# Gating a chunk of the mLSTM behind the first head of the next chunk

## The chip, the cores and the metric

The kernel runs on one core of a Trainium2 chip. The metric is the device time of one execution in microseconds (us), the median of several runs. Five engines run side by side, each with its own queue of instructions in a fixed order: PE (TensorE, matrix products, with weight loads shown apart as PEld), DVE (VectorE), ACT (ScalarE), POOL (GpSimd) and SP (SyncE, which issues most loads). ACT issues the stores.

## The reference, cut to what matters

The reference is one step of a two-layer streaming encoder. The change touches one part of layer 0, the mLSTM mixer over 16 meta tokens and 2048 prompt tokens, with 4 heads of 256 features:

```
h = num / jnp.maximum(jnp.abs(den), jnp.exp(-m))[..., None]     # per head, a row per token
...
C1 = decay[..., None, None] * C0 + jnp.einsum('bhsd,bhse->bhde', kw, v)   # state after the chunk
...
y = head_norm(h, norm_w) + skip.astype(F32) * xc
...
gated = jnp.concatenate([ya * jax.nn.silu(za), yb * jax.nn.silu(zb)], axis=-1)
```

So each token's rows are normed per head, scaled by `norm_w`, the product of `skip` and the convolved input `xc` is added (the skip product), and all of it is multiplied by the gate `zb`.

## The kernel before

The prompt is worked in chunks of 128 tokens. `phase_mlstm` (from 925 to about 1250 us of the profile) takes one unit of the meta tokens and then eight units of two chunks. In the texts below A is the first chunk of a unit and B the second. Pass i of the loop writes the score stage of unit i+1 (`ml_scores`), and then the heads of A and of B of unit i (`ml_heads`), each followed by its gating (`ml_gated`).

- **Score stage** (needs no state). `xc` is split in two float32r parts (L105 on ACT, L106 on POOL). The queries of the unit are 48 products (L111, L112, L113, 16 of each) in four PSUM tiles, copied out by ACT (L1092). For each chunk: a load of the decay rows `rw` (L1108, SP) and of the values `va` (L1114), the scaled queries `qs` (L1117, two on DVE), the keys turned in two PSUM tiles (L1125) and weighted into `kw` by ACT (L1128), the weights `w` (L1132 on ACT, L1133 on POOL), the scores in one PSUM tile (L1142) and their weighting into `p` (L1145, DVE), and last the skip product `g` (L1147, POOL).
- **Heads**, four per chunk. Products L1272 and L1274 give the head's rows in a PSUM tile `pn`; L1277 gives two tiles `pc` by which DVE (L1281) moves the state `ct`. `ml_normed` takes statistics on DVE (L1158 to L1164), a power on POOL (L1165, L1166), and ACT writes the normed rows into `yn` (L1167).
- **Gating** of a chunk. SP loads `zb` (L1175). Two groups of four turns on PE (L1180, heads 0 and 1, then 2 and 3) go to two PSUM tiles, read by two groups of four DVE instructions (L1183) that add into `g`. POOL multiplies `g` by `zb` (L1185), ACT stores (L1186).

PSUM tiles are lent by name. `pa` has three slots, shared by the four query tiles, the six tiles of keys and scores of a unit, and the four tiles of its gating; `pn` has three and `pc` two. In SBUF `yn`, `g` (`m_g`), `kw`, `p`, `qs`, `rw` and `zb` have two slots each, `xc` three: a chunk's `yn` can be written only when the chunk two before it has been turned, and its `g` only when L1185 of the chunk two before it is through. In units 2 to 5 a row of out-projection weights is staged in a slot of `zb` (L1320 to L1322); the last loads of weights (L1312) and the operands of the first tile of the out-projection take slots of `xc`.

The order of instructions in each engine's queue is not the written order. The framework lays the queues out at build time: among instructions whose operands and slots are there, the one written earlier goes first. So where a step is written decides who gets a slot that comes free, and the layout is fixed before the program runs.

Of the kernel before, what the change touches and what calls it, by code (L numbers as in the profile page):

```python
# [9 lines left out]
F32 = mybir.dt.float32  # L10
# [3 lines left out]
OP = mybir.AluOpType  # L14
# [9 lines left out]
KD = 8  # L24
# [21 lines left out]
def opn(e, name, bufs=1, side=None, psum=False):  # L46
    """open a pool that outlives the function; cls closes it"""
    if psum:
        cm = e.tc.tile_pool(name=name, bufs=bufs, space=MemoryType.PSUM, side=side, reuse_waits="tile")
    else:  # L50
        cm = P(e, name, bufs, side)
    e.cms[name] = cm
    return cm.__enter__()
# [11 lines left out]
def exp_acc(nc, pool, out, x, shape, nm):  # L65
    """out = exp(x) to float32 accuracy; x is clobbered."""
# [19 lines left out]
def log1p_acc(nc, pool, out, z, shape, nm):  # L86
    """out = log(1 + z) for 0 <= z <= 1."""
    s = pool.tile(shape, F32, name=nm + "_s")
    q = pool.tile(shape, F32, name=nm + "_q")
    p = pool.tile(shape, F32, name=nm + "_p")  # L90
    v = nc.vector
    v.tensor_scalar(s, z, 2.0, None, op0=OP.add)
    v.reciprocal(s, s)
    v.tensor_mul(s, s, z)
    v.tensor_mul(q, s, s)
    v.tensor_scalar(p, q, 1.0 / 17.0, None, op0=OP.mult)
    for k in (15.0, 13.0, 11.0, 9.0, 7.0, 5.0, 3.0):
        v.scalar_tensor_tensor(p, p, 1.0 / k, q, op0=OP.add, op1=OP.mult)
    v.scalar_tensor_tensor(out, p, 1.0, s, op0=OP.add, op1=OP.mult)
    v.tensor_scalar(out, out, 2.0, None, op0=OP.mult)  # L100


def split(nc, h, l, x, pool=False, act=True):
    """x = h + l with both parts exact in float32r."""
# [4 lines left out]
def mm3(nc, out, a, b, start, stop, **kw):  # L109
    """out (+)= a.T @ b with operands split in two parts; a, b: (h, l) tuples of APs."""  # L110
# [5 lines left out]
def token_tiles():  # L116
    """(column of the first token, tokens, kind, row)"""
# [17 lines left out]
def params(e, ps):  # L135
    """Per-feature vectors and conv histories, one row each, turned to feature-major columns."""
# [32 lines left out]
def rms_rstd(e, out, junk, x, n):  # L169
    """out [n, 1] = (mean(x^2) + eps)^-1/2 over the rows of x [n, 1024]; junk: room for the squares"""  # L170
# [6 lines left out]
def norm_u(e, ps, x, n, rs, nwb, uh, ul, pname, pbufs, keep=None):  # L177
    """x [n, 1024] token-major -> x * rs * nwb (in place), feature-major in two parts: uh, ul [128, 8, n]; keep takes
    them, half of the features at a time"""
# [13 lines left out]
def blocks_of(first, rest):  # L193
    """token tiles in blocks of tiles: (tiles, first column, columns)"""
# [8 lines left out]
def phase_in0(e):  # L203
    """norm of layer 0, S5 input and its gate; weight preparation beside it"""
# [5 lines left out]
    with P(e, "a_w") as wp, P(e, "a_sb", 2) as sb, PS(e, "a_ps") as ps:  # L210
# [37 lines left out]
        for i, bi in enumerate(seq):  # L248
# [33 lines left out]
            if i == 4:  # L282
                # the first columns of what follows
# [10 lines left out]
def prep_ml(e, sb, ps):  # L294
    """mLSTM projections folded: q~ = xc (wq wk^T) / 16, gate weights on xc and on xb"""
    nc = e.nc
    # gate weights of two heads side by side, in 32 rows each of which 8 count
# [43 lines left out]
def phase_l0(e):  # L341
    """xb, zb of layer 0, conv, values, gates; S5 beside it; the mLSTM factors"""
# [13 lines left out]
    def mtile(third, m, isz, ut, pg, parts):  # L356
        """a generator: the first block of tokens, then the rest"""
# [52 lines left out]
        # four parts side by side in the array  # L410
# [4 lines left out]
    def quarters(ut):  # L415
        """(first column, columns) of the parts of a third, from its start"""
# [3 lines left out]
    def values(h, ut, tiles, parts):  # L420
        """token-major values of a head, and what they add to the gates"""
# [32 lines left out]
    for third in range(3):  # L454
# [6 lines left out]
        if third > 0:  # L461
            # the second block takes the room of the last third's first
# [7 lines left out]
        def tile(m, isz):  # L470
            """values wait for one more tile, till their operands are split"""
# [71 lines left out]
def s5_open(e, ps):  # L543
    """discretised S5: powers of A, coefficients of B (stacked: real part over imaginary part), states"""
# [4 lines left out]
    with P(e, "s5prm", side="right") as sb:  # L549
# [52 lines left out]
        # (A - 1) / lambda  # L602
# [20 lines left out]
        # by position in the chunk: the last one has power 0  # L623
# [10 lines left out]
        # B as stored [g, p, c] -> [p twice, g, c]  # L634
# [6 lines left out]
        # states of the running streams, stacked  # L641
# [13 lines left out]
def s5_u(e, sb, q):  # L655
    """S5 input of 4 groups: rows (position, channel), two halves of 8 positions each, per group and chunk"""
# [7 lines left out]
def s5(e, ps):  # L664
    """a generator: l0 takes a piece at a time"""
# [5 lines left out]
    with P(e, "s5a", side="right") as sb:  # L671
# [31 lines left out]
        # states of the running streams  # L703
# [18 lines left out]
        # scan over the chunks of the prompt: pairs of chunks first, then the chunks between  # L722
# [8 lines left out]
        def advance(dst, src, n, g0):  # L731
            """ee[dst] += A^16 ee[src] for n chunks, every second one"""
# [39 lines left out]
    with P(e, "s5y", side="right") as sb:  # L772
        # coefficients of C; C as stored [g, c, p] -> [p twice, (g c)]; skip weights on the diagonal of lag 0
# [15 lines left out]
        # four groups of lags lie side by side in 32 rows each, the upper 16 unused  # L789
# [55 lines left out]
    # gelu, GLU, gate; the weights in the room of the normed tokens' rows  # L845
    with P(e, "s5g", side="right") as sb:
# [24 lines left out]
        def operands(b):  # L871
            """4 of the 16 positions, half the chunks"""
# [39 lines left out]
def gate_rows(e, ps):  # L912
    """running max and decay sums of the mLSTM gates; rows (slot, head): slot 0 the running streams, 1 the meta
    tokens, 2.. the chunks of the prompt. Leaves every chunk's factors."""
    nc, v = e.nc, e.nc.vector
    with P(e, "gr", side="right") as sb:
# [29 lines left out]
        # running max over the chunks of the prompt  # L946
# [3 lines left out]
        # turned to one row per head and one column per chunk, and back  # L950
# [48 lines left out]
def m_open(e, ps):  # L999
    """mLSTM factors and weights, while the in-projection still runs"""  # L1000
# [34 lines left out]
def ml_scores(e, sb, lp, hp, pt, slots):  # L1035
    """everything of a chunk that needs no state: values, queries, weighted keys, weighted scores; lp: the pool of
    what is loaded; hp: the pool of what is dropped at the end; pt: PSUM tiles by use"""
    nc, v = e.nc, e.nc.vector
    sk = e.row["ml_skip"]
# [16 lines left out]
    else:  # L1056
        kt = xc
        am = e.m.am
        if meta:
            # apart, that the next chunks' need not wait  # L1060
# [5 lines left out]
    if meta:  # L1066
        # few tokens: the weights run, and the queries are turned
# [34 lines left out]
    for i, slot in enumerate(slots):  # L1102
# [8 lines left out]
        # values with columns of ones  # L1111
# [34 lines left out]
        g = c.g = sb.tile([128, KD, 128], F32, name="m_kt" if dec else "m_g", bufs=nb(2))  # L1146
        nc.gpsimd.tensor_tensor(g[:, :, :n], c.xc, e.pc[:, :, sk:sk + 1].to_broadcast([128, KD, n]), op=OP.mult)  # L1147
# [3 lines left out]

def ml_normed(e, c, h, pn):
    """a head's rows over their normaliser, normed"""
# [16 lines left out]
def ml_gated(e, c):  # L1170
    """norm weights, gate"""
# [17 lines left out]
def ml_running(e, sb, pt):  # L1189
    """the running streams, each with its own state; a generator of one step per head and four streams. Two streams  # L1190
    fill 32 columns of the array, so that four products run side by side."""
# [5 lines left out]
    # keys and values, split  # L1197
# [8 lines left out]
    for h in range(H):  # L1206
# [6 lines left out]
        for b in range(2):  # L1213
# [12 lines left out]
            # two streams fill 32 rows of the array as well, one of them masked  # L1226
# [24 lines left out]
def ml_columns(e, sb, ptile, src, name):  # L1251
    """normaliser states out, from columns"""
# [12 lines left out]
def ml_heads(e, c):  # L1265
    """a chunk's rows, and the state after it"""
    nc, ct, n = e.nc, e.m.ct, c.n
    first = c.slot == 1  # the streams of the prompt start from nothing
# [15 lines left out]
    ml_gated(e, c)  # L1284


def phase_mlstm(e):
# [5 lines left out]
    def weights(k, r, h, l):  # L1293
        """of the out-projection"""
# [3 lines left out]
    with P(e, "m_sb", 2) as sb, PS(e, "m_ps") as ps:  # L1298
# [3 lines left out]
        nxt = ml_scores(e, sb, lp, ow0, pt, units[0])  # L1302
        for i in range(len(units)):
# [3 lines left out]
            else:  # L1307
                # the rest of the weights in the room of the last chunks' queries and keys
# [7 lines left out]
            for c in cur:  # L1316
                ml_heads(e, c)
            if 2 <= i < 6:
                # staged in line with the gates
                r = sb.tile([128, D], F32, name="m_zb", bufs=2)  # L1320
                nc.sync.dma_start(r, out_w(e)[:, i - 2, :])
                weights(i - 2, r, *(ow0.tile([128, D], F32R, name=f"wo{x}{i - 2}") for x in "hl"))  # L1322
        t = out_tiles(e)[0]
# [6 lines left out]
        # state of the prompt in the basis of k  # L1330
# [14 lines left out]
def split_weights(e, wp, src, ks, width, name, stg, sname, bufs=2):  # L1345
    """DRAM matrix [128, k, width] -> its two parts, a tile per k"""
# [16 lines left out]
def out_tiles(e):  # L1363
    """token tiles in the order of the out-projection; the meta tokens go apart"""
# [4 lines left out]
def out_operands(e, room, parts, c0, n, kind, row):  # L1369
    """gated tokens, split; room(j, "g" or "h" or "l"): tiles for a part of the features"""  # L1370
# [22 lines left out]
def phase_out0(e):  # L1393
    """out-projection of layer 0, residual; the first in-projections of layer 1"""
# [3 lines left out]
    with P(e, "o_sb", 2) as sb, P(e, "o_w") as wp:  # L1398
# [22 lines left out]
        def meta():  # L1421
            """few tokens: a quarter of the features each, side by side in the array; a generator of a step per k"""
# [20 lines left out]
        # two tiles at once while the weights come  # L1443
# [45 lines left out]
def p1_block(e, b):  # L1489
    """room for the normed tokens of a block"""  # L1490
# [35 lines left out]
def p1_plain(e, m, wt, b):  # L1526
    """128 columns of q, k, v (m < 16) or of the gate of the retention, for a block of tokens"""
# [11 lines left out]
def phase_in1(e):  # L1539
    """in-projection of layer 1; RG-LRU as its inputs come"""  # L1540
# [6 lines left out]
    with P(e, "p_ms") as sb:  # L1547
        cs = sb.tile([128, KD, 27], F32, name="p_cs", bufs=1)
        hs = sb.tile([128, KD, 9], F32, name="p_hs", bufs=1)
        # softplus(-lambda) = max(-lambda, 0) + log1p(exp(-|lambda|)), times 2 for the tanh below  # L1550
# [15 lines left out]
        # the first columns run block by block, as the normed tokens come  # L1566
# [103 lines left out]
        def values(j, wv):  # L1670
            """512 columns of v, token-major; the first block as it comes, then turned"""
# [55 lines left out]
def phase_ret(e):  # L1727
    """retention, out-projection of layer 1, final norm"""
# [3 lines left out]
    # the last columns of the in-projection run block by block; the room of the finished blocks goes to what follows  # L1732
# [25 lines left out]
    def retention(c0, n, kind, row):  # L1758
        """-> the gated parts, split, for the out-projection"""
# [26 lines left out]
        if not meta:  # L1786
# [8 lines left out]
            for h in range(H):  # L1795
                po = ps.tile([128, 256], F32, name="r_o", bufs=2)
                mm3(nc, po, hd(p, h), hd(vv, h), True, False, skip_group_check=dec)
                if dec:
                    # two streams fill 32 columns of the array: four products run side by side
# [94 lines left out]
    def load(j, ks):  # L1894
        """weights of the out-projection; those of the RG-LRU come first"""
# [146 lines left out]
```

## Time and profile before

| what | value |
|---|---|
| three runs, us | 3164.87, 3166.68, 3168.04 (median 3166.68) |
| span of the profiled execution, first to last instruction | 3164.7 us |
| PE busy over the span | 3012.2 us (95%) |
| DVE busy over the span | 1725.9 us (55%) |
| mean granted TensorE clock over the span | 0.979 of full speed |
| the mLSTM phase, 925 to 1260 us | PE busy 302.17 of 335, DVE 251.31, POOL 180.40 |

The page gives the profiled execution's span and no other time of its own; the span lies 0.2 us under the lowest of the three runs and 2.0 us under their median. A busy PE is not PE at its peak, since the ends of pipelined matmuls are modelled. "L1183" is line 1183 of the kernel before.

### The profile page before, as it was taken

What the parts mean: (1) busy time and instruction counts of PE and PEld (TensorE: products, weight loads), DVE (VectorE), ACT (ScalarE), POOL (GpSimd) and SP (SyncE); (2) the same over time, 40 slices, a digit from 0 to 9 for tenths busy, and PEclk for the clock granted to TensorE, in tenths of its full rate; (3) what the DMA queues carried; (4) which work ended last, traced back from release to release, by engine and by line L of the source; (5) the groups of instructions that cost most, each with busy time, mean ns of one, the idle gap of its engine ahead of it and who ended that gap; (6) DMA issues with size and microseconds to landing.
All of it is one profiled execution on the core that took longest, in us unless ns stands there. A gap on an engine that the chain in (4) does not pass through costs nothing.

```text
span 3164.7 us, 45082 instructions
## 1 busy us (share of the span) xinstructions
PE 3012.2 (95%) x17427; PEld 2721.5 (86%) x17427; DVE 1725.9 (55%) x3449; ACT 1059.3 (33%) x1860; POOL 905.3 (29%) x931
## 2 busy tenths in 40 slices
PE   8999978997899989999999999999999999999999
PEld 7998877987888877767799999999998897888887
DVE  4336797454447886233355666666620026666664
ACT  4223332334434443311224555555531112211211
POOL 6103434333325664121201111111110014434432
PEclk9999988999899999999999999999999999999999
DMA  7436433557463555765532111111121148544542
GB/s 215 116 84 197 126 113 103 158 165 165 115 209 108 157 156 165 233 188 170 169 129 73 51 51 51 51 51 51 49 90 63 63 147 248 148 118 131 138 122 75
DMA packets 444035, 396.36 MB, mean 125 GB/s; under 512 B 43401, under 2 KB 392786, under 8 KB 443819
## 3 DMA queue, kind: packets, MB, share of 16 engines
q1 hardware_dynamic: 333164, 268.13, 29.9%
q10 hardware_dynamic: 110654, 125.33, 11.9%
q8 instruction: 137, 2.24, 0.3%
q14 instruction: 80, 0.65, 0.1%
HBM read 262.12 MB, written 131.27 MB: 124 GB/s over the span
## 4 chain that ended last, share of the span: by engine, by line
PE 73%; DVE 15%; DMA 5%; issue 3%; ACT 2%; POOL 2%; SPq 0%; ACTq 0%; DVEq 0%; POOLq 0%
PE p_pm L112 8%; PE p_pm L111 8%; PE p_pm L113 8%; PE r_pm L113 4%; PE r_pm L112 4%; PE pm L111 4%; PE r_pm L111 4%; PE pm L113 4%; PE pm L112 4%; PE pa L111 3%; PE pa L112 3%; PE pa L113 3%; DVE xc L527 2%; PE pn L1274 1%; PE pc L1277 1%
## 5 line engine op out<-in xcount | busy, mean ns | idle before, releaser
L111 PE MATMUL p_pm<-pu,p_wh 128*128 128x384 f32 (+1 forms) x1568 | 512.1, 327 | 0.2 <-ACT pu L105 0.2
L112 PE MATMUL p_pm<-pu,p_wh 128*128 128x384 f32 (+1 forms) x1568 | 511.8, 327 | 0.0
L113 PE MATMUL p_pm<-pu,p_wl 128*128 128x384 f32 (+1 forms) x1568 | 511.3, 326 | 0.0
L111 PE MATMUL pm<-ub,wh 128*128 128x384 f32 (+1 forms) x1136 | 382.9, 338 | 9.3 <-ACT vo L435 6.1
L112 PE MATMUL pm<-ub,wh 128*128 128x384 f32 (+1 forms) x1136 | 379.7, 334 | 1.7 <-DVE ub L106 1.7
L113 PE MATMUL pm<-ub,wl 128*128 128x384 f32 (+1 forms) x1136 | 377.2, 335 | 1.6 <-POOL wl L106 1.6
L111 PEld LDWEIGHTS p_pm<-pu,p_wh 128*128 128x128 f32 x1568 | 294.2, 188 | 1.8 <-issue 1.2
L112 PEld LDWEIGHTS p_pm<-pu,p_wh 128*128 128x128 f32 x1568 | 294.6, 188 | 1.0 <-issue 0.8
L113 PEld LDWEIGHTS p_pm<-pu,p_wl 128*128 128x128 f32 x1568 | 294.5, 188 | 0.0
L111 PEld LDWEIGHTS pm<-ub,wh 128*128 128x128 f32 x1136 | 219.0, 193 | 14.6 <-ACT vo L435 6.9
L113 PEld LDWEIGHTS pm<-ub,wl 128*128 128x128 f32 x1136 | 217.6, 192 | 5.6 <-issue 3.3
L112 PEld LDWEIGHTS pm<-ub,wh 128*128 128x128 f32 x1136 | 218.7, 192 | 3.7 <-DVE ub L106 2.1
L112 PE MATMUL r_pm<-rol,r_gh 128*128 128x512 f32 x544 | 217.9, 401 | 1.3 <-POOL rol L106 0.9
L111 PE MATMUL r_pm<-roh,r_gh 128*128 128x512 f32 x544 | 218.0, 401 | 0.9 <-ACT p_o L1535 0.5
L113 PE MATMUL r_pm<-roh,r_gl 128*128 128x512 f32 x544 | 216.9, 400 | 1.1 <-DVE r_gl L106 1.1
L106 POOL TENSOR_TENSOR wl<-wr,wh 128x1024 fp32r<-128x1024 f32 x47 | 119.3, 2540 | 265.9 <-ACT wh L105 259.2
L106 POOL TENSOR_TENSOR p_wl<-p_wr,p_wh 128x1024 fp32r<-128x1024 f32 x34 | 81.8, 2408 | 383.6 <-ACT p_wh L105 373.1
L113 PEld LDWEIGHTS r_pm<-roh,r_gl 128*128 128x128 f32 x544 | 103.0, 189 | 23.0 <-DVE r_gl L106 1.6
L111 PEld LDWEIGHTS r_pm<-roh,r_gh 128*128 128x128 f32 x544 | 102.7, 189 | 22.2 <-ACT p_o L1535 0.9
L112 PEld LDWEIGHTS r_pm<-rol,r_gh 128*128 128x128 f32 x544 | 102.9, 189 | 21.7 <-POOL rol L106 1.3
L1625 DVE RECIPROCAL p_d<-p_d 128x384 f32<-128x384 f32 (+1 forms) x48 | 116.7, 2431 | 0.6
L106 POOL TENSOR_TENSOR p_xcl<-p_xc,p_xch 128x384 fp32r<-128x384 f32 (+1 forms) x48 | 46.8, 974 | 245.3 <-ACT p_xch L105 208.8
(716 smaller groups left out, 6822.8 us busy)
## 6 DMA issues: line engine op xcount, KB each, us to landing
wr<-in_ev_w_in_dram SPq DMA_DIRECT2D x47, 512.0 KB
p_wr<-in_od_w_in_dram SPq DMA_DIRECT2D x40, 512.0 KB
d_in<-p_o ACTq DMA_DIRECT2D x80, 192.0 KB
m_rw<-d_grow SPq DMA_DIRECT2D x18, 512.0 KB
s5u<-d_ua SPq DMA_DIRECT2D x32, 274.0 KB
d_v<-vo ACTq DMA_DIRECT2D x68, 128.0 KB
m_va<-d_v SPq DMA_DIRECT2D x17, 512.0 KB
d_h<-o_x ACTq DMA_DIRECT2D x17, 512.0 KB
```

The costliest lines, as they stand in the source:

```text
L106: (nc.gpsimd if pool else nc.vector).tensor_tensor(l, x, h, op=OP.subtract)
L111: nc.tensor.matmul(out, a[0], b[0], start=start, stop=False, **kw)
L112: nc.tensor.matmul(out, a[0], b[1], start=False, stop=False, **kw)
L113: nc.tensor.matmul(out, a[1], b[0], start=False, stop=stop, **kw)
L527: v.scalar_tensor_tensor(out, x(j), pc[:, m, cw + j:cw + j + 1], out, op0=OP.mult, op1=OP.add)
L1274: nc.tensor.matmul(pn[:n], c.qs[:, 2 * h + k, :n], ct[h][:, k, :], start=False, stop=k == 1)
L1277: nc.tensor.matmul(pc, c.kw[:n, h, 128 * k:128 * (k + 1)], c.va[:n, h, :], start=True, stop=True)
L1625: v.reciprocal(d[:, :n], d[:, :n])
```

## The change

The gating of a chunk leaves the end of its own `ml_heads`. It is now written after head 0 of the next chunk; for the last chunk, after the loop. So the gating of B of unit i now stands behind the score stage of unit i+2, which pass i+1 writes ahead of its heads; before, it stood ahead of that. The skip product leaves the score stage and is written at the head of its chunk's `ml_heads`. The running streams (`dec`) keep theirs where it was. No instruction is added or taken out. The rest of the diff takes away comments and docstrings.

```diff
@@ ml_scores
-    sk = e.row["ml_skip"]
...
-        g = c.g = sb.tile([128, KD, 128], F32, name="m_kt" if dec else "m_g", bufs=nb(2))
-        nc.gpsimd.tensor_tensor(g[:, :, :n], c.xc, e.pc[:, :, sk:sk + 1].to_broadcast([128, KD, n]), op=OP.mult)
+        if dec:
+            ml_skip(e, c)
         res.append(c)
     return res
 
+def ml_skip(e, c):
+    sk, n = e.row["ml_skip"], c.n
+    c.g = c.sb.tile([128, KD, 128], F32, name="m_kt" if c.dec else "m_g", bufs=1 if c.dec else 2)
+    e.nc.gpsimd.tensor_tensor(c.g[:, :, :n], c.xc, e.pc[:, :, sk:sk + 1].to_broadcast([128, KD, n]), op=OP.mult)
@@ ml_heads
-def ml_heads(e, c):
+def ml_heads(e, c, before):
     nc, ct, n = e.nc, e.m.ct, c.n
     first = c.slot == 1
+    ml_skip(e, c)
     c.yn = c.sb.tile([128, H, 256], F32, name="m_yn")
     for h in range(H):
...
         ml_normed(e, c, h, pn)
-    ml_gated(e, c)
+        if before and not h:
+            ml_gated(e, before)
@@ phase_mlstm
         nxt = ml_scores(e, sb, lp, ow0, pt, units[0])
+        before = None
         for i in range(len(units)):
...
             for c in cur:
-                ml_heads(e, c)
+                ml_heads(e, c, before)
+                before = c
...
+        ml_gated(e, before)
         t = out_tiles(e)[0]
```

## Rows read from the trace of the kernel before

**Rows 1.** The page, busy time of the engines over the span.

```profile
PE 3012.2 (95%) x17427; PEld 2721.5 (86%) x17427; DVE 1725.9 (55%) x3449; ACT 1059.3 (33%) x1860; POOL 905.3 (29%) x931
```

**Rows 2.** Windows of six units of two chunks; first row: the columns.

```profile
core 0: us, PE busy (x) PEld busy (x) DVE busy (x) ACT busy (x) POOL busy (x), PEclk, DMA share, GB/s
...
1078.10:1114.10 36.00, 32.47 (x192) 28.86 (x192) 30.81 (x89) 15.09 (x31) 22.88 (x27) 0.95 0.53 162
...
sum 215.80, PE 192.63 PEld 171.35 DVE 183.45 ACT 91.44 POOL 134.31; mean PE 32.10 PEld 28.56 DVE 30.57 ACT 15.24 POOL 22.39
```

**Rows 3.** Windows inside one unit, columns as in rows 2.

```profile
1074.80:1078.20 3.40, 0.00 (x0) 0.00 (x0) 3.40 (x8) 0.00 (x0) 2.64 (x4) 1.00 0.45 129
...
1079.80:1083.00 3.20, 3.20 (x15) 3.02 (x14) 3.20 (x7) 1.05 (x2) 2.50 (x2) 0.50 0.50 169
```

**Rows 4.** Waits of PE, 1006 to 1245 us: total, times, longest.

```profile
PE pa L111 <- DVE m_g L1183: 17.3, 5, 3.5
PE pa L1180 <- DVE m_g L1183: 3.9, 2, 3.5
```

**Rows 5.** Timeline of PE, one unit: start, us, what [idle before <- releaser].

```profile
1069.60 0.60 PE L1180 MATMUL pa<-ident,m_yn 128*128 128x128 f32 x4
...
1072.01 0.60 PE L1272 MATMUL pn<-m_va,m_p 128*128 128x258 f32 x2
...
1073.75 0.60 PE L1180 MATMUL pa<-ident,m_yn 128*128 128x128 f32 x4
...
1078.26 0.39 PE L111 MATMUL pa<-m_xch,amh 128*128 128x256 f32 x1 [3.47 <-DVE m_g L1183]
...
1095.85 2.05 PE L1142 MATMUL pa<-m_qt,m_xc 128*128 128x128 f32 x16
...
1102.97 1.03 PE L1277 MATMUL pc<-m_va,m_kw 128*128 128x258 f32 x4
```

**Rows 6.** Timeline of DVE, the same unit.

```profile
1073.32 3.73 DVE L1117 TENSOR_TENSOR m_qs<-m_qt,m_rw 128x512 f32<-128x512 f32 x2
...
1077.09 1.11 DVE L1183 SCALAR_TENSOR_TENSOR m_g<-pa,pc,m_g 128x128 f32<-128x128 f32 x4
...
1080.35 0.68 DVE L1145 TENSOR_TENSOR m_p<-pa,m_w 128x512 f32<-128x512 f32 x1
...
1081.03 1.47 DVE L1161 SCALAR_TENSOR_TENSOR m_sm<-m_sm 128x1 f32<-128x1 f32 x1
...
1092.81 1.28 DVE L1117 TENSOR_TENSOR m_qs<-m_qt,m_rw 128x512 f32<-128x512 f32 x2
```

**Rows 7.** Timeline of POOL, the same unit.

```profile
1073.09 2.36 POOL L1185 TENSOR_TENSOR m_zb<-m_g,m_zb 128x1024 f32<-128x1024 f32 x1 [3.01 <-DMA m_rw<-d_grow]
...
1080.11 2.38 POOL L1185 TENSOR_TENSOR m_zb<-m_g,m_zb 128x1024 f32<-128x1024 f32 x1 [0.19 <-DVE m_g L1183]
...
1087.36 2.90 POOL L1147 TENSOR_TENSOR m_g<-m_xc,pc 128x1024 f32<-128x1024 f32 x1
```

**Rows 8.** Timeline of ACT, the same unit.

```profile
1071.16 1.02 ACT L1167 ACTIVATE m_yn<-pn,m_sm 128x256 f32<-128x256 f32 x2 [1.91 <-issue]
...
1103.67 1.57 ACT L1128 ACTIVATE m_kw<-pa,wecol 128x256 f32<-128x256 f32 x4 [0.76 <-PE pc L1277]
```

**Rows 9.** Timeline of PE, end of the phase.

```profile
1203.56 0.70 PE L1272 MATMUL pn<-m_va,m_p 128*128 128x258 f32 x2 [0.28 <-ACT m_yn L1167]
...
1221.91 0.65 PE L1180 MATMUL pa<-ident,m_yn 128*128 128x128 f32 x4 [3.48 <-DVE m_g L1183]
...
1247.64 0.39 PE L111 MATMUL pa<-m_qt,m_xc 128*128 128x512 f32 x1
```

**Rows 10.** Timeline of SP: loads into slots of xc.

```profile
1090.29 1.91 SPq L1047 DMA_DIRECT2D m_xc<-d_xc  x1
...
1194.25 0.56 SPq L1312 DMA_DIRECT2D m_xc<-in_ev_w_out_dram  x1
```

**Rows 11.** Groups by line, 990 to 1195 us: busy, mean ns.

```profile
L1147 POOL TENSOR_TENSOR m_g<-m_xc,pc 128x1024 f32<-128x1024 f32 x12 | 27.3, 2279 | 0.0
```

## Prediction

> **What bounds the kernel now.** The page comes first: PE is busy 95% of the span [rows 1], so a change elsewhere pays only where it shortens a stretch in which PE waits or runs slowly. The windows over six units of two chunks come next. A unit lasts 35.97 us in the mean (215.80 / 6). PE is busy for 32.10 of it and DVE for 30.57 [rows 2]: both are near full, and DVE has only 5.4 us to spare. That DVE figure matters below.
>
> Third, the waits of PE. One pair stands out: the first product of the queries (L111) waits for DVE's gating (L1183), 17.3 us in five times, 3.5 at the longest; the turns L1180 wait for the same 3.9 us in two times [rows 4]. The timeline of PE shows the place. Four groups of turns run between 1069.60 and 1073.75, both chunks of the previous unit, and L111 starts at 1078.26 after 3.47 us of nothing [rows 5]. What is missing is a slot of `pa`. Of three, one holds the scores of B from 1095.85 (one unit earlier: about 1060) until DVE weights them at 1080.35; the other two hold turned rows that only L1183 can empty [rows 5, 6]. DVE is busy for all of the 3.40 us in which PE stands still [rows 3]: from 1073.32 it spends 3.73 us on two L1117, and L1183 comes at 1077.09 [rows 6].
>
> The stall has a second price. After it, from 1079.80 to 1083.00, the granted clock is 0.50, that is the lower level, 1.2 of 2.4 GHz [rows 3]. Half of 3.2 us, 1.6 us of PE work, is lost. The unit thus loses 3.47 + 1.6 = 5.1 us at this place. It occurs at five units, and at a sixth place, 1221.91, with 3.48 us before a turn [rows 4, 9]: 30 us in all that the change could at most win here.
>
> **The change part by part.** No instruction is added or removed; 17 gatings (each two groups L1180, two groups L1183, one L1185, a load L1175 on SP's queue, a store L1186 on ACT's) and 17 skip products move. Their durations stay; only order and waits can change the time. The page's PE work, 32.10 us a unit less the 1.6 of slow clock, is some 30.5 us and is the floor.
>
> Step 1, the gating of A. It is written one head later, but it stood behind the score stage of the next unit before and does so still. In the trace of before it already runs long behind B's heads, since it needs a slot of `pa` that the keys and scores of the next unit hold; ACT's four L1128, 1.57 us from 1103.67, free two of them once the last L1277 of a chunk (1102.97) has given up a slot of `kw` [rows 5, 8]. I count nothing for it.
>
> Step 2, the gating of B. Before, it was written ahead of the score stage of the unit after next; now it stands behind it. All ten `pa` tiles of that stage, ready since they need only `xc`, go first. So B's turns miss their place in the cluster before L111 and come one cluster later, when the keys of the following unit's B have given up their slots. Each cluster still has four groups, but of B and the next A in place of A and B. What stands around it differs. Before, PE had one head and some L1277 left beside the cluster (1072.01) [rows 5], and then nothing. Now the last head of a B and four heads of the next A stand right behind it. So the 3.47 us before L111 have work to cover them. I take the stall as gone, and with it the 1.6 us of slow clock. Bounds: it stays in full (0), or goes in full (-5.1 a unit).
>
> Step 3, the new wait. `yn` has two slots, so B's rows can be written only when the last B has been turned, and that is now after the cluster. Heads 0 to 2 of B fill the three slots of `pn`; head 3 waits. PE's L1272 behind `yn` is in the trace once, at 0.28 us [rows 9]; a wait of this length is not, so I build it from rows. From the last L1277: four L1128 on ACT, 1.57; two groups of turns, each 0.60 by its row and 0.43 apart when pipelined, 1.0; L1167, 0.5 (1.02 for two) [rows 5, 8]. With four handovers at about 0.1 to 0.25 (1102.97 + 0.60 plus 0.1 gives 1103.67 on ACT) that is some 3.5 us, in which PE does 0.9 us of turns: 2.6 us idle. Queued behind head 3 on PE are all heads of the next A. Bounds: nothing, if the layout gives B's turns a slot earlier; 3.5 us, if even the turns don't cover. As it is shorter than 3.47 us I take it without slow clock; with it, 1.6 more.
>
> Step 4, the skip product. Twelve of them took 27.3 us, 2.28 each on POOL [rows 11]. It needs a slot of `g`, freed by L1185 two chunks before, as it did. The cover for it is POOL's idle time, 36 - 22.4 us a unit [rows 2]; without that cover it would be 2.28 us a chunk. What is late with it: it is the last reader of `xc`, and B's is now one cluster later, so a slot of `xc` comes free up to one unit later. The load at 1090.29 [rows 10] has three slots and is used a unit on; hidden. At the end, the load of out-projection weights at 1194.25 [rows 10] would move to some 1225, a unit on, and is wanted at 1247.64 [rows 9]; I count 0, bound +5.
>
> SP's queue: L1175 moves behind loads of `rw` and `va` of the next chunk, with its product far off; 0.
>
> Sum by unit: -3.47 - 1.6 + 2.6 = -2.5 us, at six places -15. But DVE is busy 30.57 us of each unit, and 33.4 us would leave it 2.8 to spare where it has 5.4. Waits of PE for DVE in the heads must grow. Between none of the gain and all I take three fifths, as DVE keeps half of its slack: -1.5 at six places, -9 us.
>
> A row on DVE and POOL bears on step 4. Two L1117 take 1.28 us at 1092.81 and 3.73 at 1073.32, where POOL's L1185 runs from 1073.09 for 2.36: the difference, 2.45, is that product. L1161, one element wide, takes 1.47 beside the next L1185 [rows 6, 7]. The Trainium skill, "SBUF — State Buffer", section "Who interferes with whom", says that a DVE instruction with two SBUF inputs and a GpSimd instruction that reads SBUF keep each other out for the whole instruction. By that rule, with which these rows agree, it speaks against the change: the sum is the one of rival 3.
>
> **The rivals.**
> 1. The whole stall goes and no new one comes, because B's turns find a slot early: -5.1 at six places, 3136 us. Against it: the slots are spoken for [rows 5, 6].
> 2. The change doesn't do what it says. The layout, not the written order, places the turns; the cluster and its stall look the same, or what goes before L111 comes back before head 3 of B, with slow clock: -5.1 + 2.6 + 1.6, -0.9 at six places, -5 us at most, 3161 to 3168.
> 3. The skip products and L1185 fall among the small DVE instructions of the heads that now must fill PE. One hold-up of 2.28 us a unit on the chain to `yn`: +14 on the forecast's -9, 3171. For it L1161's 1.47 [rows 6]; against it, an L1147 of 2.90 at 1087.36 stood beside heads already [rows 7].
> 4. The other side, slower: the stall before L111 stays, since a cluster of four groups still stands ahead of it and DVE still empties it behind L1117, and the wait of head 3 is added: +2.6 at six places, 3182. It decides when the heads behind the cluster can't run, that is when `yn` of B is written later than the queries could start.
>
> **How the numbers follow.** The span of the profiled execution, 3164.7, against which the sum is made, lies 2.0 under the median of 3166.7; I carry differences over as they are. Forecast: 3166.7 - 9 = 3158 us, chance 0.40, own range 3150 to 3160. Rival 1: 0.08. Rival 2: 0.14. Rival 3: 0.08. Rival 4: 0.30. A change under 0.2%, 6.3 us, is about what a measurement of this kernel cannot tell from none. Faster: 0.40 + 0.08 = 0.48; same: 0.14 + 0.08 = 0.22; slower: 0.30. The range reaches from 3140, short of rival 1's end, to 3184, rival 4 with 2 us of the load at the end.
>
> **What would show it.** Step 2 is right if the five waits of L111 for L1183 are gone or under 1 us, and the first turns behind the last L1277 of a B are those of the B before it. Step 3: PE's L1272 waits for `yn` (L1167) about 2.6 us once a unit. The clock of the unit windows would be 1.00 instead of 0.95. DVE's busy time by unit should be unchanged at some 30.5 us in a unit of 34 to 35 us. The prediction is wrong if L111's waits stay beside the new one (rival 4), if DVE's busy time grows by 2 us a unit (rival 3), or if the time moved outside of 925 to 1260 us, where nothing is rewritten but the queues are laid out anew.

## Result, and the profile after

The changed kernel takes 3192.44 us (median of four runs, 3188.43 to 3200.20); the kernel before took 3167.32 us in the runs beside it. The ratio is 1.0086, 95% interval 1.0072 to 1.0100: slower by 25 us, where 9 us less was forecast and 3184 us was the upper end of the range. The profiled spans are 3186.7 and 3164.7 us.

The line numbers moved a little. In the rows of after, L1091 is the copy of the queries (before L1092), L1107 the load of `m_rw` (L1108), L1116 the query product (L1117), L1127 the weighted keys (L1128), L1131 the exponentials (L1132), L1141 the scores (L1142), L1155 the skip product (L1147), L1173 the normed rows (L1167), L1186 and L1189 the turns and the gating on DVE (L1180, L1183), L1191 the gate on POOL (L1185), L1279, L1281 and L1284 PE's products of a head (L1272, L1274, L1277), and L1288 the state update on DVE (L1281).

**Where the time went.** First the score products, the products that end a head's rows, and layer 1's first product, of before and then of after (least, median and longest ns of one, first to last start in us):

```profile
L1142 PE MATMUL pa<-m_qt,m_xc x272: 176/275/551, 941.6 to 1207.1; 128*128 128x128 f32 x128, 128*16 128x16 f32 x8
...
L1274 PE MATMUL pn<-ct,m_qs x256: 378/381/639, 962.0 to 1236.8; 128*128 128x258 f32 x128
...
L111 PE MATMUL p_pm<-pu,p_wh x1568: 282/334/446, 1602.3 to 2659.2; 128*128 128x384 f32 x160, 128*128 128x272 f32 x36
```

```profile
L1141 PE MATMUL pa<-m_qt,m_xc x272: 187/275/550, 936.3 to 1221.8; 128*128 128x128 f32 x128, 128*16 128x16 f32 x8
...
L1281 PE MATMUL pn<-ct,m_qs x256: 378/381/639, 959.3 to 1262.1; 128*128 128x258 f32 x128
...
L111 PE MATMUL p_pm<-pu,p_wh x1568: 282/334/445, 1622.3 to 2678.3; 128*128 128x384 f32 x160, 128*128 128x272 f32 x36
```

From the first scores to the last it was 265.5 us and is 285.5; I call this stretch the score units. From the first scores to the first `p_wh` product it was 660.7 us and is 686.0. So of 25.3 us, 20.0 lie in the units and 5.3 between the last scores and layer 1. In that second stretch the last product of a head comes 40.3 us behind the last scores where it came 29.7, and from it to `p_wh` it is 360.2 us where it was 365.5: in these profiles the 5.3 us are lost in the last heads, not behind them. The first scores start 5.3 us earlier after, ahead of anything that was rewritten; `p_wh` itself takes about as long as before (1056.0 against 1056.9 us). These two distances are used for every kernel below.

**What stayed and what went.** The page's busy time [rows 1], a window of one unit and its sum over four units [rows 2], and the waits of PE, 1006 to 1245 us [rows 4]:

```profile
PE 3018.7 (95%) x17427; PEld 2722.6 (85%) x17427; DVE 1717.3 (54%) x3449; ACT 1055.8 (33%) x1860; POOL 901.3 (28%) x931
```

```profile
1052.57:1090.70 38.13, 31.79 (x193) 27.41 (x192) 28.91 (x88) 14.62 (x31) 21.65 (x27) 1.00 0.51 152
...
sum 154.37, PE 128.80 PEld 111.07 DVE 113.63 ACT 58.01 POOL 86.12; mean PE 32.20 PEld 27.77 DVE 28.41 ACT 14.50 POOL 21.53
```

```profile
PE pc L1284 <- DVE ct L1288: 18.6, 7, 3.5
PE pa L111 <- ACT m_qt L1091: 9.5, 6, 1.8
PE pa L1186 <- ACT m_kw L1127: 5.9, 6, 1.0
PE pa L1186 <- DVE m_g L1189: 4.0, 7, 1.1
PE pa L1186 <- ACT m_yn L1173: 2.3, 1, 2.3
```

The old stall, L111 behind the gating, 17.3 us in five [rows 4], is gone, and the clock of this window is 1.00 where it was 0.95. (In one of the four windows, from 1128.66 to 1168.86, it is still 0.96.) Yet this unit takes 38.13 us, and the mean of the four 38.6 (154.37 / 4), where it was 35.97. In the stall's place PE has several waits of 1 to 3 us, for the state update, the query copies and the keys. Where engines wait for one another in turn, the chain of waits says what they wait for in the end. This is the chain of after inside one unit (start, us, what):

```profile
1055.60 0.80 DVE ct L1288 x2
1056.42 5.54 DMA m_rw<-d_grow
1061.98 1.29 DVE m_qs L1116 x2
1063.40 0.41 DVE ct L1288
1063.86 1.14 PE pc L1284 x4
1064.99 1.97 PE pa L1141 x16
1066.96 0.89 PE pc L1284 x4
1067.93 0.85 ACT m_kw L1127 x2
1068.83 0.67 PE pa L1186 x4
1069.52 3.19 DVE m_g L1189 x12
1072.71 0.78 DVE ct L1288 x2
1073.52 5.89 DMA m_rw<-d_grow
...
1080.04 0.68 ACT m_w L1131 x2
...
1081.23 0.38 PE pa L111
...
1093.93 0.80 DVE ct L1288 x2
1094.74 4.96 DMA m_rw<-d_grow
```

It is a loop. `m_rw` has two slots, one a chunk. A chunk's slot is held from its load to the last state update of its heads, which reads the decay from it. From 1056.42 to 1094.74, 38.3 us, two loads stand in the chain with 5.54 + 5.89 = 11.4 us. The chain of before has no load in it from 1040 to 1100 us. From 1006 to 1200 us the loads of `m_rw` are 6.8% of the chain in before and 23.3% in after; the two of before are these:

```profile
1139.92 5.64 DMA m_rw<-d_grow
1193.38 7.59 DMA m_rw<-d_grow
```

DVE's and ACT's queues show the two steps that closed the loop (timeline: start, us, what, [idle before <- releaser]):

```profile
1061.98 1.29 DVE L1116 TENSOR_TENSOR m_qs<-m_qt,m_rw 128x512 f32<-128x512 f32 x2 [2.37 <-DMA m_rw<-d_grow]
...
1063.32 0.87 DVE L1288 SCALAR_TENSOR_TENSOR ct<-ct,m_rw,pc 128x258 f32<-128x258 f32 x2
...
1069.52 3.19 DVE L1189 SCALAR_TENSOR_TENSOR m_g<-pa,pc,m_g 128x128 f32<-128x128 f32 x12 [3.94 <-PE pa L1186]
1072.63 0.86 DVE L1288 SCALAR_TENSOR_TENSOR ct<-ct,m_rw,pc 128x258 f32<-128x258 f32 x2
```

```profile
1067.93 1.57 ACT L1127 ACTIVATE m_kw<-pa,wecol 128x256 f32<-128x256 f32 x4 [4.61 <-PE pc L1284]
...
1079.43 1.28 ACT L1131 ACTIVATE m_w<-m_rw,acol 128x128 f32<-128x128 f32 x4 [7.57 <-DMA m_rw<-d_grow]
...
1080.62 0.56 ACT L1091 COPY m_qt<-pa 128x512 f32<-128x512 f32 x1
```

The product for B's last state update ends on PE at 1067.84 (row of 1066.80 below). The update itself, L1288, runs only at 1072.63: ahead of it in DVE's queue stand twelve instructions L1189, two groups of four of the B before and one of the A behind it, for which DVE waits 3.94 us and then works 3.19. Only then is the slot free, and the load is issued at 1073.52. When it lands, 5.9 us later, ACT has waited 7.57 us with L1131, with the query copies L1091 queued behind, and PE's L111 behind those. In the other half of the unit the load of 1056.42 makes DVE's L1116 wait with L1288 behind it, and PE's L1284 behind that:

```profile
1063.86 1.14 PE L1284 MATMUL pc<-m_va,m_kw 128*128 128x258 f32 x4 [3.23 <-DVE ct L1288]
...
1066.80 1.04 PE L1284 MATMUL pc<-m_va,m_kw 128*128 128x258 f32 x4
1068.83 1.38 PE L1186 MATMUL pa<-ident,m_yn 128*128 128x128 f32 x8 [0.99 <-ACT m_kw L1127]
...
1071.19 0.60 PE L1279 MATMUL pn<-m_va,m_p 128*128 128x258 f32 x2
...
1081.23 0.38 PE L111 MATMUL pa<-m_xch,amh 128*128 128x256 f32 x1 [1.43 <-ACT m_qt L1091]
```

In before, the corresponding load was issued at 1068.19, ahead of the gatings of that cluster, the first of which ran at 1070.34:

```profile
1068.19 0.61 SPq L1108 DMA_DIRECT2D m_rw<-d_grow  x1
```

The waits for `m_rw` show the difference (total, times, longest; 925 to 1262 us), before:

```profile
ACT m_w L1132 <- DMA m_rw<-d_grow: 20.6, 15, 4.4
DVE m_qs L1117 <- DMA m_rw<-d_grow: 4.7, 3, 2.5
```

and after:

```profile
ACT m_w L1131 <- DMA m_rw<-d_grow: 83.8, 15, 8.7
...
DVE m_qs L1116 <- DMA m_rw<-d_grow: 21.5, 14, 2.6
```

### The profile page after: what moved, and what is told of

Same layout as the page of the kernel before. It is cut to its first block, busy times and chain, and to the rows that moved or that the text cites. A ratio compares the mean times of both kernels' runs of the same rounds, so it can differ in the third digit from the quotient of the medians.

```text
span 3186.7 us, 45083 instructions
## 1 busy us (share of the span) xinstructions
PE 3018.7 (95%) x17427; PEld 2722.6 (85%) x17427; DVE 1717.3 (54%) x3449; ACT 1055.8 (33%) x1860; POOL 901.3 (28%) x931
## 4 chain that ended last, share of the span: by engine, by line
PE 54%; DVE 7%; DMA 3%; issue 1%; ACT 1%; POOL 0%; SPq 0%; ACTq 0%; DVEq 0%; POOLq 0%
PE p_pm L112 8%; PE p_pm L113 8%; PE p_pm L111 8%; PE r_pm L112 4%; PE r_pm L113 4%; PE r_pm L111 4%; PE pa L111 3%; PE pa L112 3%; PE pa L113 3%; DMA m_rw<-d_grow 2%; DVE p_d L1636 1%; DVE p_xc L525 1%; PE r_o L1838 1%; DVE p_xc L527 1%; DVE m_g L1189 1%
## 5 line engine op out<-in xcount | busy, mean ns | idle before, releaser
L111 PE MATMUL p_pm<-pu,p_wh 128*128 128x384 f32 (+1 forms) x1568 | 512.1, 327 | 0.2 <-ACT pu L105 0.2
L111 PE MATMUL pm<-ub,wh 128*128 128x384 f32 (+1 forms) x1136 | 383.2, 338 | 8.3 <-ACT vo L435 5.0
L111 PEld LDWEIGHTS p_pm<-pu,p_wh 128*128 128x128 f32 x1568 | 294.2, 188 | 1.8 <-issue 0.8
L111 PEld LDWEIGHTS pm<-ub,wh 128*128 128x128 f32 x1136 | 219.3, 193 | 13.2 <-ACT vo L435 5.9
L111 PE MATMUL r_pm<-roh,r_gh 128*128 128x512 f32 x544 | 217.7, 401 | 0.5 <-ACT p_o L1546 0.5
L111 PEld LDWEIGHTS r_pm<-roh,r_gh 128*128 128x128 f32 x544 | 102.7, 189 | 21.5 <-ACT p_o L1546 0.9
```

The costliest lines, as they stand in the source:

```text
L111: nc.tensor.matmul(out, a[0], b[0], start=start, stop=False, **kw)
```

## Experiments

Theory 1: with B's turned rows late, the loads of `m_rw` come late, because the heads hold its two slots; the unit waits for the loads. Theory 2: the two slots of `yn` hold B's heads behind the cluster, and that is the loss. Theory 3, the third rival: the moved skip product disturbs DVE. Except in `a_only`, every edit below also gave the queues of the engines a new order, so that what a slot is worth and what the new order is worth are not held apart by the times alone; the traces are read beside them. Each kernel was timed in three rounds beside before (medians 3166.1 to 3167.3 us). "Units" and "to `p_wh`" are the two distances above, each from one profile.

| kernel | us | ratio to before, 95% interval | units | to `p_wh` |
|---|---|---|---|---|
| before | 3167 | 1 | 265.5 | 660.7 |
| after | 3192 | 1.0072 to 1.0100 | 285.5 | 686.0 |
| `a_only` | 3164 | 0.9978 to 0.9997 | 265.4 | 660.3 |
| after, `yn` 3 slots | 3185 | 1.0047 to 1.0080 | 276.8 | 678.4 |
| after, `m_rw` 3 slots | 3184 | 1.0043 to 1.0073 | 267.5 | 678.7 |
| after, both 3 slots | 3151 | 0.9936 to 0.9970 | 254.1 | 648.4 |
| before, `yn` 3 slots | 3193 | 1.0052 to 1.0097 | 289.8 | 688.5 |
| before, `m_rw` 3 slots | 3168 | 0.9989 to 1.0014 | 265.0 | 664.3 |
| before, both 3 slots | 3153 | 0.9954 to 0.9976 | 250.6 | 646.7 |

**One part alone.** `a_only` gates A behind B's head 0 and has the skip product in the heads, as after, but gates B where before did:

```diff
+            before = None
             for c in cur:
                 ml_heads(e, c, before)
                 before = c
+            ml_gated(e, before)
...
-        ml_gated(e, before)
         t = out_tiles(e)[0]
```

> The changed kernel, but B's gating back at the end of B's own heads; A's gating behind B's first head and the skip product in the heads stay as changed. Theory 1 (the score stage's DMA loads of m_rw come late once B's heads are held behind the cluster of turns, and stand at the head of DVE's and ACT's queues) and theory 2 (two slots of m_yn hold B's heads) both need B's gating to be late: 3167 us, no change against before. Theory 3 (the moved skip product disturbs DVE): still about 3190.

Measured 3163.81 us. Its instructions stand in the same order on all five engines as in before, so the 3 us are no effect of the edit, although the interval leaves out 1: differences of this size between two kernels are not read below. With B's gating in its old place the whole loss is gone. Theory 3 is not settled by this run, as the skip products keep their old place in POOL's queue in it; it falls with `yn3_rw3` below, where they stand as in after and the time is 16 us under before.

**The two slots, in after.** One more slot each (for `m_rw` also at the two other places that use the name), then both:

```diff
-    c.yn = c.sb.tile([128, H, 256], F32, name="m_yn")
+    c.yn = c.sb.tile([128, H, 256], F32, name="m_yn", bufs=3)
...
-        rw = c.rw = lp.tile([128, 2, H, 128], F32, name="m_rw", bufs=nb(2))
+        rw = c.rw = lp.tile([128, 2, H, 128], F32, name="m_rw", bufs=nb(3))
```

> The changed kernel with a third slot of m_yn, so that B's heads no longer wait for the turns of the B before. Theory 2: the 20 us of the six units come back, about 3172 us (the tail's 12 may stay, 3180), unit period 36. Theory 1: the loads of m_rw still wait for two slots, so part of it at most, 3180 to 3190, and DVE's L1116 and ACT's L1131 still wait for m_rw. Theory 3: 3190.

> The changed kernel with a third slot of m_rw, so that each load of the decay rows can be issued a chunk earlier. Theory 1: the waits of L1116 and L1131 for m_rw (21.5 and 83.8 us before the end of the phase) go to under 10 us together, the unit falls from 38.1 to about 36 us, 3172 us. Theory 2: the heads are held by m_yn whatever the load does, 3188 to 3192. Theory 3: 3190.

> The changed kernel with a third slot of both m_yn and m_rw. Theories 1 and 2: no worse than the better of the two single ones; if each holds a part of the loss, better than both, 3160 to 3170, since the old stall before L111 stays gone. Theory 3: 3190.

Measured 3184.74, 3184.26 and 3150.55 us. In the units theory 1 holds: with a third slot of `m_rw` they take 267.5 us, 18 of the 20 us lost; a third slot of `yn` gives 8.7. In the total each alone gives back only 8 us, and the intervals still touch that of after. With `m_rw` free, the scores run ahead but the heads don't: the last product of a head comes 47.6 us behind the last scores (after 40.3, before 29.7), and from the last scores to `p_wh` it is then 411.2 us (678.7 - 267.5), 10.7 more than in after. That the slots of `yn` hold the heads there is concluded from the kernel with both, where the 47.6 is 30.6. With `yn` free, DVE and ACT still wait 14.8 and 21.8 us for `m_rw`. Both together give 42 us and beat before by 16. Neither theory alone explains the loss: each names one of two holds on the same heads.

**The same slots in before.** Is the late gating worth anything, or are the slots?

> The kernel before with the third slots of m_yn and m_rw, which in the changed kernel together gave 3150.6 us, 16 under before. If those slots only lift what the change itself had made (theories 1 and 2), the old stall of L111 behind the gating stays and nothing is won: 3160 to 3168. If the slots would have helped in either form, and the late gating of B is worth nothing in itself: about 3150.

> The kernel before with the third slot of m_rw alone. Both doublings cost far more than slack allows (44 us before, 29 us after), so the kernel before too waits for m_rw. Theory 4: before is held by m_rw alone, 3153 us here as with both slots; the change adds a second hold, the slots of m_yn, so that each slot alone returned little. Theory 5: both slots are needed in before as well, 3163 to 3167.

> The kernel before with the third slot of m_yn alone. Theory 4: m_yn holds nothing in before, since B's rows are turned ahead of the next score stage; m_rw holds it as it did, 3163 to 3170 us. If m_yn is the hold in before too: 3153.

Measured 3153.05, 3168.22 and 3192.98 us. With both slots before and after are alike: the intervals overlap, and whether the late gating is worth the 2.5 us between the medians stays open. What wins is there without the late gating. Theory 4 is wrong, as the third slot of `m_rw` alone does nothing for the time of before; theory 5 holds. Yet that kernel, `before_rw3`, has hardly any of the old stall left (waits of PE, 925 to 1262 us):

```profile
PE pa L111 <- DVE m_g L1183: 0.2, 1, 0.2
```

So 17 us of PE's waits for the gating went without a gain: other waits came in their place, above all L1277 for the state update, 12.6 us in nine times (4.8 in four in before), and the keys L1125 for L1145, 8.0 in three (none in before). The miss is `before_yn3`, which I expected to do nothing: it is as slow as after. With a third slot the order of the queues changes too, and the trace looks like that of after: the stall of L111 is down to 0.9 us, `m_rw` is waited for longer than in before, and its loads are 31.2% of the chain from 1006 to 1200 us (before 6.8%):

```profile
ACT m_w L1132 <- DMA m_rw<-d_grow: 34.4, 15, 4.9
DVE m_qs L1117 <- DMA m_rw<-d_grow: 23.5, 12, 4.9
...
PE pa L111 <- DVE m_g L1183: 0.9, 2, 0.5
```

So the loss doesn't need the late gating: in both kernels it came where the stall was gone while `m_rw` had two slots that the heads hold.

**Doubling the load.**

```diff
         nc.sync.dma_start(rw.rearrange("p a h t -> p (a h t)"),
                           bass.AP(tensor=e.grow.tensor, offset=e.grow.offset + r0 * 128,
                                   ap=[[0, 128], [NR * 128, 2], [1, H * 128]]))
+        nc.sync.dma_start(rw.rearrange("p a h t -> p (a h t)"),
+                          bass.AP(tensor=e.grow.tensor, offset=e.grow.offset + r0 * 128,
+                                  ap=[[0, 128], [NR * 128, 2], [1, H * 128]]))
```

> The kernel before with each chunk's load of the decay rows m_rw issued twice into the same tile. In before DVE and ACT wait 30 us in all for these loads, off the path. Theory 1: the slack covers much of a load about 3 us later, 3170 to 3185. If theory 1 is wrong, this and the same doubling in the changed kernel cost alike.

> The changed kernel with each chunk's load of m_rw issued twice into the same tile. Theory 1: the two late loads of each unit lie on the path, each lands about 3 us later, so 4 to 6 us a unit at seven units, 3220 to 3235, more than twice what the doubling costs before. Theory 2 (m_yn alone): as much as in before, 3195 to 3205.

Measured 3211.43 us (1.0130 to 1.0180) and 3220.48 us (1.0152 to 1.0191): the doubling costs 44 us in before and 28 in after. I expected the opposite. Before is not free of the loop; it stands at its edge: two loads are in its chain from 1006 to 1200 us already, and with the doubled load they are 19.7% of it instead of 6.8%. The order of the queues changed too. How much of the 44 us that makes, whether the second copies hold up other loads, and why after loses less, stays open. The load of 1068.19 is awaited in before too, by ACT, with nothing of it in the chain:

```profile
1073.16 1.28 ACT L1132 ACTIVATE m_w<-m_rw,acol 128x128 f32<-128x128 f32 x4 [0.98 <-DMA m_rw<-d_grow]
```

**Who holds the slot, and whose wait costs.** `rwcol` copies the four decays that the state update needs out of `m_rw`, so that the heads no longer hold a slot:

```diff
+        cd = c.cd = lp.tile([128, H], F32, name="m_cd", bufs=4)
+        nc.gpsimd.tensor_copy(cd, rw[:, 1, :, 127])
...
-                nc.vector.scalar_tensor_tensor(ct[h][:, k, :], ct[h][:, k, :], c.rw[:, 1, h, 127:128], pc,
+                nc.vector.scalar_tensor_tensor(ct[h][:, k, :], ct[h][:, k, :], c.cd[:, h:h + 1], pc,
```

`rw01` has the two rows in tiles of their own, each with its own load; row 0 goes to the exponentials, row 1 to the query product and the state update:

```diff
-            rw = c.rw = lp.tile([128, 2, H, 128], F32, name="m_rw", bufs=nb(2))
+            rw = [lp.tile([128, H, 128], F32, name=x, bufs=2) for x in ("m_r0", "m_rw")]
+            c.rw = rw[1]
...
```

> The changed kernel; m_rw keeps its two slots, but the last column that the state update needs is copied into a tile of four columns in the score stage, so that a slot of m_rw is free when the scores are done and no longer when the heads are. If what makes the loads late is that the heads hold the slots (theory 1), this does in the units what a third slot did: first to last score about 267 us instead of 285, total about 3184 or less. If the loads are late for another reason, as the changed kernel: 3190.

> The changed kernel with the two rows of m_rw in tiles of their own, loaded apart: the row that ACT's exponentials read (83.8 us of waits) has slots that the heads don't hold, the row that DVE's query product reads (21.5 us of waits) is held as before. If ACT's wait, with the query copies behind it, is the costly one: units 267 to 275 us, total 3175 to 3185. If DVE's wait, with the state update behind it, is: 3188 or more.

> rwcol with the third slot of m_yn. Theory 1 with theory 2: as with third slots of both, 3150 us, at 3.9 KB per partition less; if the copy itself or its place hurts, up to 3165.

> The changed kernel with three slots of m_yn and four of m_rw. DVE and ACT still waited 42 us in all for m_rw with three slots, off the path or on it. If on it: 3140 to 3147; if the loads are covered with three: 3150, no change against three.

`rwcol`: 3184.49 us (1.0042 to 1.0076), units 264.5 us, as with a third slot: in the units it is the heads' hold on the slot that makes the loads late, as theory 1 says. `rw01`: 3187.14 us (1.0047 to 1.0077), units 270.4 us, while DVE still waits for its row, 17.8 us, and no wait of ACT for its row is left. So most of the units' loss, 15 of 20 us, went with ACT's wait. The edit also halves each load, to 256 KB, so the shorter load of the row that is still held may have a part in it: the loads in its chain from 1006 to 1200 us take 3.40 to 4.74 us. The total, 5 us less than in after with intervals that overlap, missed my 3175 to 3185. `yn3_rwcol`: 3171.64 us (1.0006 to 1.0027), 21 us short of the third slot. The rows show a likely reason, not tested by itself: the copy waits for the load at the head of POOL's queue, where POOL's part of the norm goes as well. In `rwcol` this wait is 25.1 us in nine times. In `yn3_rwcol` it is the first of these rows (total, times, longest); the second is PE's wait for the normed rows, which with both third slots is 3.4 us in six times:

```profile
POOL m_cd L1121 <- DMA m_rw<-d_grow: 16.0, 4, 11.8
PE pn L1282 <- ACT m_yn L1176: 11.1, 9, 2.8
```

`yn3_rw4`: 3154.30 us (0.9946 to 0.9976), no better than three slots. Of the 42.3 us for which ACT's exponentials and DVE's query product wait for `m_rw` with three slots, 25.4 are left; the 17 that went gained nothing that can be measured.

**The end of the phase.** `tail6` has the changed order, but gates B at the end of its own heads once the last score stage is reached:

```diff
                 before = c
+            if i >= 6:
+                ml_gated(e, before)
+                before = None
...
-        ml_gated(e, before)
         t = out_tiles(e)[0]
```

> The changed kernel, but the units from the last score stage on gate B at the end of its own heads, as before; the five units earlier stay as changed. If the tail's 12 us of loss come from B's heads and slots of m_xc held up to the end, 8 to 12 us come back, about 3180. If the tail only inherits the late heads of the units ahead, at most 4 us, 3188 or more.

Measured 3192.51 us (1.0063 to 1.0104), no change. From the last scores to `p_wh` its profile has 394.5 us (682.2 - 287.7; before 395.2, after 400.5), but its units 2.2 more than after. One profile of each doesn't settle such 6 us, and the kernel doesn't tell whether late slots of `xc` cost the 5.3. The trace of after does: PE's first product of the out-projection (L111) follows the last product of a head, at 1262.1, without a wait, so its operands were there:

```profile
1262.86 0.48 PE L111 MATMUL pa<-woh,m_xc 128*128 128x512 f32 x1
```

What is late there are the last heads, and the chain of after has two loads of `m_rw` ahead of them, of 5.48 us from 1210.40 and of 5.54 from 1229.09.

## Why the prediction was wrong

**Step 1** (A's gating, nothing) and the nothing for the **skip product** in step 4: right when these are the only edits; the order on the queues doesn't change by them.

**Step 2** (the stall before L111 and the slow clock go): right in what happens. The five waits are gone, the clock is 1.00 in three of four units (0.96 in the other), and the first turns behind the last L1284 of a B, at 1068.83, are those of the B before. Its price was not to be had: in `before_rw3` the stall is gone as well, and the time is that of before. With both third slots both kernels are 14 to 16 us under before, half of the 30 us that were counted at most.

**Step 3** (a new wait of head 3 of B, 2.6 us) is the step that failed. The chain that I built, keys, turns, normed rows, is in the trace: L1127 at 1067.93, L1186 at 1068.83, and head 3 at 1071.19, 3.35 us after the last L1284 ended (1067.84); PE's wait there is 0.99 + 0.49 us, and the direct wait of its L1279 for `yn`, which I had put at 2.6 us a unit, is 0.4 us in one time in the whole phase. But I followed only PE's queue: "queued behind head 3 on PE are all heads of the next A". Behind the turned rows on DVE stands B's last state update; behind that the slot of `m_rw`; behind the slot a load of 5 to 6 us; and the wait for that load stands at the head of ACT's queue, with the query copies behind. The prediction names the queues of SP and counts the moved L1175 there as nothing, and asks of the skip product's slots what they hold, but never of `m_rw`'s. Step 2 has the same gap: it calls the score stage's tiles "ready since they need only `xc`", but the score tiles are emptied only with the exponentials of L1131, and the query tiles by copies that stand behind L1131 on ACT, and L1131 waits for `m_rw`. The unit became 38.6 us in the mean, +2.6, not -1.5: 20 us over the units.

**Step 4**, the slots of `xc`: the weights load of 1194.25 [rows 10] comes at 1205.16, not at the 1225 that was estimated, and the first operands of the out-projection at 1231.70 (before 1197.23).

```profile
1205.16 0.38 SPq L1321 DMA_DIRECT2D m_xc<-in_ev_w_out_dram  x1
...
1231.70 0.52 SPq L1388 DMA_DIRECT2D m_xc<-d_ya  x1
```

I had counted 0, bound +5. The 0 holds as far as PE shows: its first product on these operands, at 1262.86, waits for nothing. The 5.3 us that the stretch behind the last scores cost more have the size of the bound by chance; they lie in the last heads.

**The range.** It reached to rival 4, and the time is 8 us above its end. Rival 4 comes nearest, 3182, but by a wrong mechanism: the old stall didn't stay, so a time within the range would have been luck. Rival 1 falls: the whole stall went, but new waits came. Rival 2 falls: neither the stall nor its place stayed.

**Rival 3** falls as a cause: DVE is busy for 28.4 us of a unit in the mean, less than the 30.57 of before. The hold-up itself is to be seen again. Two L1116 take 1.29 us at 1061.98 and 2.25 at 1079.43, where POOL's gate, from 1078.15 for 2.38, still runs for 1.10 us:

```profile
1079.43 2.25 DVE L1116 TENSOR_TENSOR m_qs<-m_qt,m_rw 128x512 f32<-128x512 f32 x2 [1.23 <-DMA m_rw<-d_grow]
```

The difference, 0.96, is about that overlap. By the Trainium skill, "SBUF — State Buffer", section "Who interferes with whom", a DVE instruction with two SBUF inputs contends with a GpSimd instruction that reads SBUF; these rows agree with it. The hold-up is too small here to decide, and it was there before [rows 6, 7].

## What to carry to other kernels

When an instruction is moved behind a wait, follow every in-order queue on which its parts stand, not only that of the bounding engine: list what is queued behind each part, which tile slots those instructions give up, and which loads wait for the slots. A slot that is held from a load to the end of the work on it makes a loop, whose length is the load plus all that the holder waits for; compare it with the period before a stall elsewhere is removed, since it may be the next bound by a few us. Where two holds are near one another, freeing either alone may show little, as it did here, and it takes both together to see what they cost. And where each edit makes the framework lay the queues out anew, the time of one edit doesn't tell a slot from an order: read the chain of waits of each kernel beside it.

## What the runs showed of the hardware

The load of the decay rows, 512 KB into 128 partitions, stood in the chain of after with 4.96 to 6.06 us from issue to the first reader between 1035 and 1095 us. A second copy of it per chunk cost before 44 us, though DVE's and ACT's waits for this load came to 25.3 us in all in before and its chain from 1006 to 1200 us had just two of the loads in it (5.64 and 7.59 us): here the total of waits for a transfer did not tell what a longer transfer would cost.
